# RG-LRU gates of a hybrid decoder block: one matmul per 64-channel block, two blocks in two row groups of the array

## The chip, the cores and the metric

The kernel runs on one core of a Trainium2 chip. The metric is the device time of one launch in microseconds (us). Times of single instructions come from one profiled execution of the kernel; the time that is forecast is the median of unprofiled runs.

## The reference: what is computed

One decoder layer for 1024 tokens of width 1024, all in float32. One input projection feeds three mixers (RWKV-7, RG-LRU, GLA), whose outputs are concatenated into one output projection, followed by a SwiGLU feed-forward part and a final norm. The change touches the gates of the RG-LRU mixer alone:

```python
def rglru_mixer(p, conv_w, conv_b, wa, ba, wx, bx, lam, norm_g):
    xb, gate = _split(p, LRU_SIZES)
    xc = causal_depthwise_conv(xb, conv_w, conv_b)
    xblk = xc.reshape(bsz, t, LRU_BLOCKS, HEAD)
    gate_r = jax.nn.sigmoid(jnp.einsum('btnc,ncd->btnd', xblk, wa).reshape(bsz, t, LRU_WIDTH) + ba)
    gate_i = jax.nn.sigmoid(jnp.einsum('btnc,ncd->btnd', xblk, wx).reshape(bsz, t, LRU_WIDTH) + bx)
    ...
    y = h * jax.nn.gelu(gate.astype(f32))
    y = rms_norm(y.reshape(bsz, t, LRU_BLOCKS, HEAD), norm_g.reshape(LRU_BLOCKS, HEAD))
```

There are 8 blocks of 64 channels. `wa` and `wx` are 64x64 per block, so both gate projections are block-diagonal.

## The kernel before, in words

Channels lie on the 128 partitions, tokens on the free axis, in two halves of 512 tokens. The program has two large stages. In the first (to about 530 us) each half goes through the input projection, the three mixers and the output projection; in the second (to the end) the feed-forward part runs as many 128x512 matmuls (L861, L1124). Weights of the projections come from HBM as float32, are split on ACT and DVE into two parts (`wh`, `wl`, L104 and L105), and each product takes three matmuls (L133, helper `mm3`).

The source gives steps an order (the list `ORDER`, with lead times in `AHEAD`), but what order each engine's instructions stand in is decided by a list scheduler with costs of its own, when the program is built. A change of a few instructions can therefore move many others. All engines then run their queues in that order. SP issues nearly all DMAs.

The RG-LRU mixer is `lru_mix` (L613 and on), called four times: `L00` and `L01` for the first half, `L10` and `L11` for the second, each for two groups of 128 channels (`j` = 0, 1), so for eight groups in all. Each group holds two blocks of 64 channels. For a group the convolution gives `c` (L628 to L630). The gate weights come as a tile `lw` of 128 x 2 x 128 (L625), block-diagonal with zeros outside the two blocks. Two full-array matmuls (L634) give the two gates into two PSUM banks from the pool `px` (two buffers), and one tanh each (L635) takes them out, the first into `y`, the second into the tile `g`. From there ACT and DVE go on: L641, L644, L646, L647, a square root (L649), L650, the scan over tokens (L651), L653, a square (L655), a sum per block on PE (L174), L657; then `lru_fin` (L661, L663, L666), the split of `y` (L104, L105) and the output projection, which reads the RG-LRU channels first (list `KO`).

Float32 matmuls run as two passes on PE; the products of L133 with their split operands run as one. Matmuls that use part of the array are marked in the profile by active rows and columns: `64*128` is half of the rows (one of two row groups) and all columns. `hs(r)` and `ops(r)` are the lower and upper 64 partitions and the reverse.

Of the kernel before, what the change touches and what calls it, by code (L numbers as in the profile page):

```python
# [11 lines left out]
F32 = mybir.dt.float32  # L12
F32R = mybir.dt.float32r
AF = mybir.ActivationFunctionType
# [4 lines left out]
P = 128  # L19
# [49 lines left out]
def hybrid_block(tc, xT, vec, cst, w_in, w_gk, w_ups, lru_w, gk_up, w_out, w_gu, w_dn, outT):  # L69
    nc = tc.nc  # L70
    V, G, S, PE = nc.vector, nc.gpsimd, nc.scalar, nc.tensor

    with ExitStack() as ctx:
# [16 lines left out]
        bah = cp.tile([P, 8], F32, name="bah")  # L90
# [56 lines left out]
        gl = rp.enter_context(tc.tile_pool(name="gl", bufs=1, side="right"))  # L147
# [12 lines left out]
        def mix_ps():  # L160
            return ps_.tile([P, HT], F32, name="px", bufs=2)
# [122 lines left out]
        hs = lambda hh: slice(64 * hh, 64 * hh + 64)  # L284
        ops = lambda hh: slice(64 * (1 - hh), 64 * (1 - hh) + 64)
# [327 lines left out]
        def lru_mix(p, pp, y):  # L613
            it = [(j, 2 * p + j, xb, gate) for j, (xb, gate) in enumerate(pp)]
            out = lambda i: y[:, 2 + i, 3:]
            xc, ig, tt = [], [], []
            for j, i, xb, gate in it:
                ge = unit(2 + j)
                S.activation(out=ge, in_=gate, func=AF.Square, scale=math.sqrt(0.044715))
                plus1(ge, ge, gate)  # L620
                S.activation(out=ge, in_=ge, func=AF.Tanh, scale=math.sqrt(2.0 / math.pi))
                plus1(gate, ge, gate)
            for j, i, xb, gate in it:
                lw = gl.tile([P, 2, P], F32, name="lw", bufs=2)
                nc.sync.dma_start(out=lw, in_=lru_w[:, i])  # L625
                c = unit(j)
                cw = lambda n: vc("cw", 4 * n + i)
                S.activation(out=c, in_=xb[:, 0:HT], func=AF.Identity, bias=vc("cb", i), scale=cw(0))  # L628
                for n in range(1, 4):
                    V.scalar_tensor_tensor(out=c, in0=xb[:, n : n + HT], scalar=cw(n), in1=c, op0=ALU.mult, op1=ALU.add)  # L630
                g = unit(2 + j)
                for w, t, b in ((0, out(i), 0), (1, g, 4)):
                    ps = mix_ps()
                    PE.matmul(out=ps, lhsT=lw[:, w], rhs=c, start=True, stop=True)  # L634
                    S.activation(out=t, in_=ps, func=AF.Tanh, bias=bah[:, b + i : b + i + 1], scale=0.5)  # L635
                plus1(g, g, c)
                xc.append(c)
                ig.append(g)
            for j, i, xb, gate in it:
                t = unit(4 * (1 - j))  # L640
                S.activation(out=t, in_=out(i), func=AF.Tanh, scale=cdec[:, i : i + 1], bias=cdec[:, i : i + 1])  # L641
                tt.append(t)
            for j, i, xb, gate in it:
                S.activation(out=out(i), in_=out(i), func=AF.Exp, scale=ncdec[:, i : i + 1], bias=ncdec[:, i : i + 1])  # L644
                sq = unit(1)
                S.activation(out=sq, in_=out(i), func=AF.Square)  # L646
                V.scalar_tensor_tensor(out=tt[j], in0=sq, scalar=1.0, in1=tt[j], op0=ALU.add, op1=ALU.mult)  # L647
            for j, i, xb, gate in it:
                S.activation(out=tt[j], in_=tt[j], func=AF.Sqrt, scale=0.25)  # L649
                V.tensor_tensor(out=ig[j], in0=ig[j], in1=tt[j], op=ALU.mult)  # L650
                V.tensor_tensor_scan(out=tt[j], data0=out(i), data1=ig[j], initial=lstate[:, i : i + 1], op0=ALU.mult, op1=ALU.add)  # L651
                S.copy(out=lstate[:, i : i + 1], in_=tt[j][:, HT - 1 : HT])
                V.tensor_tensor(out=out(i), in0=tt[j], in1=gate, op=ALU.mult)  # L653
                sq = unit(2 + j)
                S.activation(out=sq, in_=out(i), func=AF.Square)  # L655
                ps = head_sum(sq, blk, mix_ps)
                V.tensor_scalar(out=gate, in0=ps, scalar1=1.0 / 256, scalar2=1e-6, op0=ALU.mult, op1=ALU.add)  # L657
# [421 lines left out]
        for f in range(PRE, NF):  # L1079
            if f >= KF:  # L1080
                r = hidden_room(f - KF)
# [86 lines left out]
        a, b = A.__getitem__, B.__getitem__  # L1168
# [20 lines left out]
        b = B.__getitem__  # L1189
# [53 lines left out]
        r = spread(rstd(Q2, acc1[:, Q2]))  # L1243
# [34 lines left out]
def _lay(i):  # L1278
    f = lambda n: np.asarray(i[n])[0]
    v = np.zeros((P, NV), np.float32)  # L1280

    def put(n, a):
        a = np.asarray(a)
        w = a.size // P
        v[:, VEC[n] : VEC[n] + w] = a.reshape(w, P).T

    put("g1", f("norm1_g"))
    put("g2", f("norm2_g"))
    put("gf", i["final_norm_g"])
    put("mu", f("rw_mu"))  # L1290
    for n, k in (("w0", "rw_w0"), ("a0", "rw_a0"), ("kk", "rw_k_k"), ("ka", "rw_k_a"), ("rk", "rw_r_k"), ("lng", "rw_ln_g"), ("lnb", "rw_ln_b"),
                 ("cw", "lru_conv_w"), ("cb", "lru_conv_b"), ("ba", "lru_ba"), ("bx", "lru_bx"), ("lam", "lru_lam"), ("lg", "lru_norm_g"), ("gkb", "gla_gk_b")):
        put(n, f(k))
    put("gg", np.tile(f("gla_norm_g"), 2))
    v[:, VEC["eps6"]] = 1e-6
    v[:, VEC["epsln"]] = 64e-5
    bp, b4 = np.arange(P) // 32 % 2, np.arange(P) // 8 % 4
    v[:, VEC["hm"] : VEC["hm"] + 2] = np.arange(P)[:, None] // 32 % 2 == np.arange(2)[None]
    v[:, VEC["b0"]] = b4 == 2 * bp
    v[:, VEC["b1"]] = b4 == 2 * bp + 1  # L1300

    w_in = f("w_in")
    swap = lambda w, ax: np.take(w, np.r_[0:64, 128:192, 64:128, 192:256], axis=ax)
    cols = np.concatenate([w_in[:, : 2048 + 512], swap(w_in[:, 2048 + 528 :], 1)], 1)
    tiled = lambda w: np.ascontiguousarray(w.reshape(w.shape[0] // P, P, w.shape[1] // P, P).transpose(2, 1, 0, 3))
    lw = np.zeros((P, 4, 2, P), np.float32)
    for b in range(8):
        s = slice(64 * (b % 2), 64 * (b % 2) + 64)
        lw[s, b // 2, 0, s] = f("lru_wa")[b]
        lw[s, b // 2, 1, s] = f("lru_wx")[b]  # L1310
    return (
        np.ascontiguousarray(np.asarray(i["x"])[0].T).reshape(NK, P, T),
        v,
        _constants(),
        tiled(cols),
        np.ascontiguousarray(w_in[:, 2560:2576].reshape(8, P, 16).transpose(1, 0, 2)),
        np.concatenate([np.concatenate([f("rw_w_up"), f("rw_a_up")], 0), f("rw_g_up")], 1),
        lw,
        np.concatenate([f("gla_gk_up")] * 2, 0),
        tiled(np.concatenate([f("w_out")[:768], swap(f("w_out")[768:], 0)], 0))[:, :, KO],  # L1320
        np.stack([tiled(f("ffn_w_gate")), tiled(f("ffn_w_up"))]),
        np.ascontiguousarray(f("ffn_w_down").reshape(NF, P, NK, P)),
    )
# [15 lines left out]
```

## Time and profile before

| what | before |
|---|---|
| median of 3 runs | 1205.6 us (1205.58 to 1206.74) |
| profiled execution, its own time | 1207.51 us |
| span of that execution | 1205.7 us |
| PE busy | 1159.4 us, 96% of the span |
| DVE, ACT, POOL busy | 820.5, 557.5 and 182.6 us |
| DMA moved | 225.52 MB, 187 GB/s on average |
| mean granted clock of PE | 0.992 |

The span runs from the first to the last instruction; the execution's own time has what lies around it as well, 1.8 us here. Busy shares are averages over stages: what bounds a stage is read from the waits and the order of that stage. A busy PE is the union of its matmul records, whose ends are modelled, so the distance from one start to the next is used below for what a matmul costs.

### The profile page before, as it was taken

Reading aid. Unit: us, or ns where it says so; the run is one execution under the profiler, and the core shown is the slowest. Engines: PE = TensorE matmul, PEld = TensorE weight load, DVE = VectorE, ACT = ScalarE, POOL = GpSimd, SP = SyncE. Lnnn points to the kernel's source line nnn. Section 1 sums busy time; section 2 is a strip of 40 time slices with the busy share of each in tenths; the row PEclk is TensorE's granted clock in tenths of the full one; section 3 lists DMA queues with packets and bytes.
Section 4 is the critical chain, followed back from the end, with each engine's and each line's share of the span. In section 5 each row is a group of like instructions: output and inputs, shape, how many; then the busy total and the mean of one; then the engine's idle time right before and its main releaser. Section 6 shows DMA issues by size and latency. Waiting matters only on the chain.

```text
span 1205.7 us, 18433 instructions
## 1 busy us (share of the span) xinstructions
PE 1159.4 (96%) x6550; PEld 906.5 (75%) x6550; DVE 820.5 (68%) x1513; ACT 557.5 (46%) x972; POOL 182.6 (15%) x141
## 2 busy tenths in 40 slices
PE   8899999999999999988899899999999999999996
PEld 4676667677776677766788778888888878888886
DVE  6878797887759676378978664356655475555775
ACT  7445734864541457365433234333333344444542
POOL 0000000000000000000036455454555400000000
PEclk9999999999999999999999999999999999999998
DMA  9865444343333268873699853245454798665422
GB/s 312 291 231 194 141 147 133 90 157 108 130 123 96 87 219 290 273 258 114 190 324 341 283 194 99 96 131 186 146 176 152 268 357 296 196 194 171 128 88 70
DMA packets 125213, 225.52 MB, mean 187 GB/s; under 512 B 13985, under 2 KB 17345, under 8 KB 125121
## 3 DMA queue, kind: packets, MB, share of 16 engines
q1 hardware_dynamic: 124432, 223.78, 55.1%
q8 instruction: 51, 0.84, 0.3%
q10 hardware_dynamic: 688, 0.57, 0.1%
q14 instruction: 42, 0.34, 0.1%
HBM read 149.84 MB, written 74.45 MB: 186 GB/s over the span
## 4 chain that ended last, share of the span: by engine, by line
PE 62%; DVE 15%; ACT 10%; DMA 9%; issue 3%; SPq 1%; POOL 0%; DVEq 0%; ACTq 0%; POOLq 0%
PE mm L861 24%; PE mm L1124 17%; PE mm L133 12%; DVE x L854 2%; DMA x<-w_dn_dram 2%; DMA wd<-x 1%; PE pi L368 1%; DMA wr<-w_in_dram 1%; DMA wr<-w_gu_dram 1%; ACT L663 1%; DVE wl L105 1%; PE pi L408 1%; DVE x L822 1%; DMA parts<-wl 1%; DVE u L651 1%
## 5 line engine op out<-in xcount | busy, mean ns | idle before, releaser
L133 PE MATMUL mm<-xl,wh 128*128 128x512 f32 x420 | 169.6, 404 | 0.0
L133 PE MATMUL mm<-xh,wh 128*128 128x512 f32 x400 | 162.8, 407 | 3.8 <-ACT wh L104 2.9
L133 PE MATMUL mm<-xh,wl 128*128 128x512 f32 x400 | 163.0, 408 | 0.3 <-DVE wl L105 0.3
L104 ACT CAST wh<-wr 128x512 fp32r<-128x512 f32 x133 | 82.0, 619 | 126.5 <-PE mm L861 37.7
L104 ACT CAST vh<-wr 128x512 fp32r<-128x512 f32 x81 | 50.2, 622 | 103.7 <-PE mm L1124 39.1
L133 PEld LDWEIGHTS mm<-xh,wh 128*128 128x128 f32 x400 | 75.4, 188 | 27.1 <-issue 6.1
L133 PEld LDWEIGHTS mm<-xl,wh 128*128 128x128 f32 x420 | 79.0, 188 | 21.9 <-issue 6.4
L105 POOL TENSOR_TENSOR wl<-wr,wh 128x512 fp32r<-128x512 f32 x36 | 53.0, 1472 | 279.9 <-ACT wh L104 265.2
L133 PEld LDWEIGHTS mm<-xh,wl 128*128 128x128 f32 x400 | 75.3, 188 | 22.6 <-issue 5.8
L1124 PE MATMUL mm<-ft,wh 128*128 128x512 f32 x264 | 81.5, 389 | 0.0
L1124 PE MATMUL mm<-ft,vh 128*128 128x512 f32 x264 | 81.3, 389 | 0.0
L854 DVE TENSOR_TENSOR x<-x 128x512 f32<-128x512 f32 x71 | 57.8, 824 | 29.2 <-DMA x<-hd 15.8
L105 DVE TENSOR_TENSOR wl<-wr,wh 128x512 fp32r<-128x512 f32 x97 | 66.3, 685 | 14.2 <-ACT wh L104 13.7
L417 POOL MEMSET ri<- 128x256 f32 x8 | 2.5, 312 | 391.3 <-DVE ri L402 389.3
L1124 PEld LDWEIGHTS mm<-ft,wh 128*128 128x128 f32 x264 | 49.6, 188 | 10.3
L1124 PEld LDWEIGHTS mm<-ft,vh 128*128 128x128 f32 x264 | 49.5, 188 | 10.2
L105 POOL TENSOR_TENSOR vl<-wr,vh 128x512 fp32r<-128x512 f32 x36 | 50.6, 1406 | 37.6 <-ACT vh L104 36.1
L1124 PE MATMUL mm<-ft,wl 128*128 128x512 f32 x132 | 51.3, 389 | 0.0
L1124 PE MATMUL mm<-ft,vl 128*128 128x512 f32 x132 | 51.3, 389 | 0.0
L104 ACT CAST wh<-ws 128x512 fp32r<-128x512 f32 x33 | 20.4, 622 | 50.9 <-PE mm L861 41.0
L105 POOL TENSOR_TENSOR wl<-ws,wh 128x512 fp32r<-128x512 f32 x27 | 38.4, 1424 | 34.6 <-ACT wh L104 26.9
L105 POOL TENSOR_TENSOR vl<-ws,vh 128x512 fp32r<-128x512 f32 x27 | 37.2, 1376 | 35.7 <-ACT vh L104 35.7
(498 smaller groups left out, 2901.0 us busy)
## 6 DMA issues: line engine op xcount, KB each, us to landing
wr<-w_gu_dram SPq DMA_DIRECT2D x108, 256.0 KB, 3.1
parts<-wh SPq DMA_DIRECT2D x60, 256.0 KB, 3.1
parts<-wl SPq DMA_DIRECT2D x60, 256.0 KB, 3.1
wh<-parts SPq DMA_DIRECT2D x57, 256.0 KB, 2.7
wl<-parts SPq DMA_DIRECT2D x57, 256.0 KB, 2.9
wr<-w_in_dram SPq DMA_DIRECT2D x44, 256.0 KB, 3.9
x<-w_dn_dram SPq DMA_DIRECT2D x44, 256.0 KB, 4.5
wd<-x SPq DMA_DIRECT2D x44, 256.0 KB, 3.9
```

The costliest lines, as they stand in the source:

```text
L104: S.copy(out=hi, in_=src)
L105: lo_eng.tensor_tensor(out=lo, in0=src, in1=hi.bitcast(F32), op=ALU.subtract)
L133: PE.matmul(out=ps, lhsT=ww[:, kk], rhs=xx(k), start=first, stop=last)
L368: PE.matmul(out=pgs[hh][:, n * P : n * P + P], lhsT=BKn[hs(hh), nn, 64 * hh : 64 * hh + 128], rhs=ARn[hs(hh), nn], start=True, stop=True)
L408: PE.matmul(out=ps[hs(hh), n * w : n * w + w], lhsT=lhs(hh, n), rhs=rhs(hh, n), start=True, stop=True)
L417: G.memset(hi(Zt), 0.0)
L651: V.tensor_tensor_scan(out=tt[j], data0=out(i), data1=ig[j], initial=lstate[:, i : i + 1], op0=ALU.mult, op1=ALU.add)
L663: S.activation(out=gate, in_=gate, func=AF.Exp, scale=-0.5)
L822: V.scalar_tensor_tensor(out=xk, in0=xk, scalar=vc("g2", k), in1=rs, op0=ALU.mult, op1=ALU.mult)
L854: eng.tensor_tensor(out=out, in0=a, in1=b, op=op)
L861: PE.matmul(out=ps, lhsT=ww[:, kk], rhs=xx, start=first and kk + i == 0, stop=kk == len(xc) - 1 and i == 2, skip_group_check=True)
L1124: PE.matmul(out=out(m), lhsT=ww[:, m], rhs=xx, start=first and open_(m) and k + i == 0, stop=k == KF - 1 and i == 2, skip_group_check=True)
```

## The change

The weight tile holds 128 x 2 x 64 numbers: the 64 partitions of a block have both of the block's gate matrices side by side in 128 columns (in the upper block in reverse order). Each group of 128 channels now has one matmul per block with 64 rows and 128 columns: block 0 in the lower row group into one bank, block 1 in the upper row group into the other. A bank so holds both gates of one block, each on 64 partitions, and four tanh of 64 partitions take them out in place of two of 128. The tanh of the second gate read the partitions opposite to those they write, since block 0's second gate lies on the upper partitions.

```diff
-                lw = gl.tile([P, 2, P], F32, name="lw", bufs=2)
+                lw = gl.tile([P, 2, 64], F32, name="lw", bufs=2)
                 nc.sync.dma_start(out=lw, in_=lru_w[:, i])
...
                 g = unit(2 + j)
-                for w, t, b in ((0, out(i), 0), (1, g, 4)):
-                    ps = mix_ps()
-                    PE.matmul(out=ps, lhsT=lw[:, w], rhs=c, start=True, stop=True)
-                    S.activation(out=t, in_=ps, func=AF.Tanh, bias=bah[:, b + i : b + i + 1], scale=0.5)
+
+                pg = [mix_ps(), mix_ps()]
+                for r in range(2):
+                    PE.matmul(out=pg[r], lhsT=lw[hs(r)].rearrange("p a b -> p (a b)"), rhs=c[hs(r)], start=True, stop=True)
+                for r in range(2):
+                    S.activation(out=out(i)[hs(r)], in_=pg[r][hs(r)], func=AF.Tanh, bias=bah[hs(r), i : i + 1], scale=0.5)
+                for r in range(2):
+                    S.activation(out=g[hs(r)], in_=pg[r][ops(r)], func=AF.Tanh, bias=bah[hs(r), 4 + i : 5 + i], scale=0.5)
                 plus1(g, g, c)
...
-    lw = np.zeros((P, 4, 2, P), np.float32)
+    lw = np.zeros((P, 4, 2, 64), np.float32)
     for b in range(8):
-        s = slice(64 * (b % 2), 64 * (b % 2) + 64)
-        lw[s, b // 2, 0, s] = f("lru_wa")[b]
-        lw[s, b // 2, 1, s] = f("lru_wx")[b]
+        s, r = slice(64 * (b % 2), 64 * (b % 2) + 64), b % 2
+        lw[s, b // 2, r] = f("lru_wa")[b]
+        lw[s, b // 2, 1 - r] = f("lru_wx")[b]
```

In the changed kernel the matmuls are on L635 and the tanh on L637 and L639; lines behind them are four higher. The order of the instructions moves on PE, DVE, ACT and SP from early in the input projection to some way into the feed-forward part; behind that it is the same.

**Order 1.** PE, the first group of `L00`, in the midst of the input projection (L133; L378 transposes one row group for RWKV). Before, and then of the change:

```order
L133 MATMUL mm<-xh_155,wh 128x512
L133 MATMUL mm<-xl_156,wh 128x512
L634 MATMUL px<-u_1163,lw 128x512 x2
L378 MATMUL pi<-ct,BK 128x64 x8
L133 MATMUL mm<-xh_155,wl 128x512
```

```order
L133 MATMUL mm<-xl_152,wh 128x512
L133 MATMUL mm<-xh_151,wl 128x512
L635 MATMUL px<-u_1163,lw 128x512 x2
L133 MATMUL mm<-xh_155,wh 128x512
L133 MATMUL mm<-xl_156,wh 128x512
```

The two gate matmuls follow each other in both; they now stand alone between full-array matmuls.

**Order 2.** PE, the last group of `L11`, shortly before the output projection of the second half. Before, and then of the change:

```order
L634 MATMUL px<-u_4897,lw 128x512
L133 MATMUL mm<-xh_4258,wh 128x512
L133 MATMUL mm<-xl_4259,wh 128x512
L133 MATMUL mm<-xh_4258,wl 128x512
L133 MATMUL mm<-xh_4262,wh 128x512
L634 MATMUL px<-u_4897,lw 128x512
```

```order
L635 MATMUL px<-u_4911,lw 128x512
L133 MATMUL mm<-xl_4271,wh 128x512
L133 MATMUL mm<-xh_4270,wl 128x512
L133 MATMUL mm<-xh_4274,wh 128x512
L133 MATMUL mm<-xl_4275,wh 128x512
L635 MATMUL px<-u_4911,lw 128x512
```

Four full-array matmuls stand between the two gate matmuls in both.

**Order 3.** ACT, the two groups of `L11`. Before, and then of the change:

```order
L635 ACTIVATE y_101<-px,bah 128x512
L641 ACTIVATE u_4910<-y_101,cdec 128x512
L635 ACTIVATE u_4887<-px,bah 128x512
L644 ACTIVATE y_101<-y_101,ncdec 128x512
L104 CAST wh<-wr 128x512
L635 ACTIVATE y_101<-px,bah 128x512
L641 ACTIVATE u_4912<-y_101,cdec 128x512
L644 ACTIVATE y_101<-y_101,ncdec 128x512
L635 ACTIVATE u_4902<-px,bah 128x512
```

```order
L637 ACTIVATE y_101<-px,bah 64x512
L639 ACTIVATE u_4899<-px,bah 64x512
L637 ACTIVATE y_101<-px,bah 64x512
L639 ACTIVATE u_4899<-px,bah 64x512
L645 ACTIVATE u_4926<-y_101,cdec 128x512
L104 CAST wh<-wr 128x512
L648 ACTIVATE y_101<-y_101,ncdec 128x512
L637 ACTIVATE y_101<-px,bah 64x512
L639 ACTIVATE u_4916<-px,bah 64x512
L637 ACTIVATE y_101<-px,bah 64x512
L639 ACTIVATE u_4916<-px,bah 64x512
```

Four tanh of 64 partitions now stand where two of 128 stood, and the next step of the group (L641, now L645) comes behind all four, where it came behind the first.

## Rows read from the trace of the kernel before

**Rows 1.** Busy us by stretch: PE, PEld, DVE, ACT, POOL; clock, DMA share, GB/s.
```profile
60.00:460.00 400.00, 394.06 (x3083) 285.72 (x3082) 309.97 (x721) 208.77 (x353) 2.50 (x8) 1.00 0.44 146
460.00:500.00 40.00, 39.06 (x215) 29.98 (x214) 24.78 (x44) 22.86 (x32) 0.00 (x0) 1.00 0.76 257
...
530.00:600.00 70.00, 57.99 (x236) 45.55 (x235) 63.67 (x105) 38.70 (x66) 0.00 (x0) 0.95 0.46 149
...
700.00:1205.00 505.00, 492.01 (x2293) 411.40 (x2291) 289.48 (x430) 203.66 (x367) 132.25 (x99) 0.99 0.52 172
```
**Rows 2.** PE's waits from 60 to 460: us in total, times, longest.
```profile
PE pi L301 <- DVE Tt L426: 1.6, 2, 1.1
...
PE px L174 <- ACT u L655: 0.3, 1, 0.3
```
**Rows 3.** Timeline of PE around the first gate matmuls: start us, us, instruction, count.
```profile
84.67 1.88 PE L634 MATMUL px<-u,lw 128*128 128x512 f32 x4
86.49 0.71 PE L378 MATMUL pi<-ct,BK 64*128 64x64 f32 x8
```
**Rows 4.** Timeline of PE where two matmuls of each row group meet, RWKV's L301 and L309.
```profile
26.43 0.48 PE L301 MATMUL pi<-pw,ups 64*128 64x256 f32 x1 [0.77 <-ACT pw L279]
26.44 0.48 PE L309 MATMUL pi<-pw,ups 64*128 64x256 f32 x1
26.75 0.38 PE L301 MATMUL pi<-pw,ups 64*128 64x256 f32 x1
...
26.96 0.37 PE L301 MATMUL pi<-pw,ups 64*128 64x256 f32 x1
...
27.18 0.38 PE L301 MATMUL pi<-pw,ups 64*128 64x256 f32 x1
...
27.50 0.50 PE L133 MATMUL mm<-xh,wl 128*128 128x512 f32 x1
27.83 0.39 PE L133 MATMUL mm<-xh,wh 128*128 128x512 f32 x1
28.06 0.40 PE L133 MATMUL mm<-xl,wh 128*128 128x512 f32 x1
```
**Rows 5.** Timeline of PE where a row group begins behind the input projection.
```profile
337.94 0.39 PE L133 MATMUL mm<-xh,wl 128*128 128x512 f32 x1
338.26 1.13 PE L309 MATMUL pi<-pw,ups 64*128 64x256 f32 x4
```
**Rows 6.** Tanh of 128 and of 64 partitions by line: ns min/median/max, first and last start.
```profile
L635 ACT ACTIVATE y<-px,bah x8: 668/678/711, 86.1 to 455.3; 128x512 f32<-128x512 f32 x8
L279 ACT ACTIVATE pw<-pw x2: 612/622/632, 25.7 to 230.6; 64x512 f32<-64x512 f32 x2
```
**Rows 7.** A group of table loads on ACT: busy us, mean ns, idle before.
```profile
L649 ACT ACT_TABLE_LOAD x4 | 5.1, 1283 | 0.1
```
**Rows 8.** Timeline of ACT, last group of `L11` to its split `y`.
```profile
455.28 0.68 ACT L635 ACTIVATE y<-px,bah 128x512 f32<-128x512 f32 x1
...
470.71 0.63 ACT L655 ACTIVATE u<-y 128x512 f32<-128x512 f32 x1 [1.19 <-DVE y L653]
...
481.95 0.62 ACT L104 CAST y<-y 128x512 fp32r<-128x512 f32 x1 [0.82 <-DVE y L666]
```
**Rows 9.** Timeline of PE: that group's sum, and the first matmul reading its `y`.
```profile
473.74 1.02 PE L174 MATMUL px<-u,ct 128*128 128x512 f32 x2
...
484.69 0.39 PE L133 MATMUL mm<-y,wh 128*128 128x512 f32 x1
```
**Rows 10.** The start by stretch, columns as in rows 1.
```profile
20.00:30.00 10.00, 9.19 (x42) 6.49 (x40) 6.61 (x14) 6.63 (x14) 0.00 (x0) 1.00 1.03 356
30.00:40.00 10.00, 7.26 (x24) 4.97 (x24) 5.09 (x12) 7.03 (x14) 0.00 (x0) 0.83 0.86 313
```
**Rows 11.** DMA issues: queue, count, KB each, us to landing.
```profile
lw<-lru_w_dram SPq DMA_DIRECT2D x8, 128.0 KB, 2.3
```
**Rows 12.** PE's waits from 530 to 600, columns as in rows 2.
```profile
PE mm L861 <- ACT ft L803: 4.2, 1, 4.2
PE mm L861 <- DVE q_t2l L105: 3.3, 2, 1.8
```

## The prediction, made before the changed kernel ran

> **What bounds the kernel now.** I read the table of busy time by stretch first, since the change lies between 60 and 460 us. PE is busy in 394.06 of those 400 us, in 39.06 of the next 40, and in 492.01 of the last 505 [rows 1]. PE is the bound nearly everywhere. The exception is 530 to 600 us, the opening of the feed-forward part, where PE has 57.99 of 70 us and DVE 63.67, and the mean granted clock is 0.95 [rows 1]: two waits of 4.2 and 3.3 us stand there [rows 12]. Then I read PE's waits in the stretch of the change: the largest is 1.6 us, for RWKV, and its wait for an RG-LRU result is 0.3 us in all [rows 2]. ACT is busy in 208.77 of those 400 us [rows 1]. So a pass taken from PE is worth its own time, and work added to ACT is hidden as long as PE still has other matmuls queued ahead of what waits for it. Last I read the timelines for prices.
>
> **PE: the passes.** The two gate matmuls of a group are four passes of 512 columns; from the first to the next work is 86.49 - 84.67 = 1.82 us [rows 3], of which about 0.09 is the change of tiling priced below, so 0.43 us a pass and 1.73 us a group. The trace has a pair in two row groups, at 256 columns: L301 and L309 start 0.01 us apart, and each stream goes on every 0.22 us as if alone [rows 4]. At 512 columns I take 0.43 us a pass, two passes side by side, 0.87 us a group, if the two matmuls stand next to each other. They do in six of the eight groups, as in order 1; each saves 0.86 us, 5.2 us in all. In the last group they are four matmuls apart, as in order 2, and nothing overlaps. In one group of `L01` a matmul of another tiling (L450) stands between them; the second then runs beside L301, which before ran beside L309, so nothing is gained there either. Passes: -5.2 us.
>
> **PE: the changes of tiling.** Going into a row group and coming back is not free. From the last L133 to the first tiled pass it is 338.26 - 337.94 = 0.32 us [rows 5], where two L133 lie 0.23 apart [rows 4]; from the first to the second tiled pass it is 0.32 where the next are 0.22 apart; from the last tiled pass to L133 it is 0.32 in place of 0.22; from that L133 to the next 0.33 in place of 0.23 [rows 4]. That is four times 0.10, so 0.2 us for each change of tiling. I counted, over the whole PE order, the places where one matmul's tile size differs from the one before: 252 before, 275 now. Of the 23 more, 14 come from the gates (order 1 shows a pair that now has one on either side), and 9 from other tiled matmuls that the scheduler put in other places. 23 x 0.2 = +4.6 us. Passes and tiling together: -0.6 us. Most of what the row groups give is taken back.
>
> **ACT.** A tanh of 64 partitions takes 0.62 us, one of 128 takes 0.68 [rows 6]; half the partitions save next to nothing. So 32 for 16 adds 16 x 0.65 = 10.4 us, and ACT's order has three more table loads (58, was 55) of 1.28 us each [rows 7], 3.9 us. These 14.3 us have PE's work as cover: ACT has nearly half of the stage free. Where the cover is thin, the next step of the group waits for two more tanh, 1.3 us (order 3), the casts of weights (L104) that PE needs are queued behind them, and both `px` banks are held until the third and fourth tanh, so the next group's gate matmuls wait longer. The thinnest place I found is behind `L11`. Before, the square of the last group was done at 470.71 + 0.63 = 471.34 and PE took it up at 473.74, 2.4 us later; its `y` was split at 482.57 and read at 484.69, 2.1 us later [rows 8, 9]. With the same prices PE's order now holds 1.2 us less work between the last gate matmul and the first one that reads that `y` (27.1 us, was 28.3). So 2.1 us of slack meet 1.2 + 1.3 us: a wait of 0.4 us. The other three calls lie amid the input projection. I take +1.5 us for all four. Bounds: 0, if all is covered, and 4 x 1.3 = 5.2, if each call shows one group's delay.
>
> **DMA.** Each of the eight loads of `lw` is 64 KB in place of 128 [rows 11]. Two are issued at the start, where the DMA engines are full (1.03 and 0.86 of their time, at 356 and 313 GB/s) and PE is not (9.19 and 7.26 of 10) [rows 10]: 131 KB at 356 GB/s is -0.4 us. The other six are hidden. SP issues as many DMAs as before. DVE and POOL have the same instructions.
>
> **The moved order.** Almost every engine's order moves, the opening of the feed-forward part too. I take 0 for it. The two waits there [rows 12] may each go or grow, and the clock's 0.95 over 70 us is some 7 us at 1.2 GHz, 3.5 us lost [rows 1]; I bound the term by 4 us either way.
>
> **Sum**: -0.6 + 1.5 - 0.4 + 0 = +0.5 us. The profiled execution took 1207.5 us, which would become 1208.0; the median of the runs shown is 1205.6, 1.9 lower, so I forecast 1206.1. A measurement of this kernel tells about 0.2% from no change, 2.4 us: no change is 1203.2 to 1208.0.
>
> **Rivals.**
> - *Faster, because changing the tiling costs nothing.* All eight groups save 0.86 us, 6.9 in all, with the DMA's 0.4: 1198.3. For it: the two streams really run side by side [rows 4]. Against it: the four 0.10 us around them [rows 4, 5], and order 2. The Trainium skill, page "TensorE: Matmul & The Clock Gate", section "Measured speedup vs the span model", prices a pack at one matmul and about 4 ns for each further tile; by it this rival would hold. The trace agrees on the start (0.01 us) and not on what stands before and behind.
> - *Faster by the moved order.* Waits at the opening of the feed-forward part shrink, or the slow-clock stretch goes: 4 us less, 1202. Nothing in the profile speaks for one sign.
> - *Slower, because the row groups don't overlap: the change doesn't do what it says.* If matmuls start strictly in order, the second block's first pass waits for the first block's second, and a pair takes three passes in place of two: 6 x 0.43 = 2.6 us given back, 1208.7. It decides if the second block starts a whole pass behind. Against it: both L301 matmuls stand ahead of both L309 in PE's order, and L309 still started 0.01 us behind the first pass of L301 [rows 4]. The Trainium skill, same page, section "The mechanism", states that matmuls start and end in strict order, with no reordering; by it this rival would hold, and the row disagrees.
> - *Slower, because the gate chain becomes the bound.* The place is behind the gates of each call, above all `L11`; the price is 5.2 us in place of 1.5, so 1209.8. It decides where the added tanh and the shorter cover pass the slack of 2.1 to 2.4 us [rows 8, 9]. For it: the slack is small, and the scheduler laid it out by its own costs. Against it: PE's 0.3 us of waiting for this chain [rows 2].
> - *Slower by the moved order*, at the same place as its faster twin: 4 us more, 1210.
>
> **How the numbers follow.** Forecast (within 0.2%): 0.40. Free tiling 0.10 and a luckier order 0.15 make faster 0.25. No overlap 0.05, gate chain 0.20 and a worse order 0.10 make slower 0.35. The range takes the sum with the order's 4 us either way and a part of the gate chain's bound above: 1201.0 to 1211.0; free tiling, and both upper bounds at once, lie outside.
>
> **What would show it.** Right: gate passes (64*128) that start in pairs 0.01 us apart in six groups, 0.43 us from pass to pass; 0.3 us steps into and out of them; 32 tanh near 0.65 us; ACT busier by 14 us; PE's waits for RG-LRU results between 60 and 500 us up by 1 to 2 us. Wrong: pairs 0.43 us apart (no overlap), steps of 0.23 us (free tiling), or a wait above 2 us at L174 or at the first output matmuls of the second half (gate chain). If the time moves by more than 2.4 us and the stretch before 500 us doesn't account for it, the moved order was mis-sized.

## The result: 1218.1 us, 1% slower

| | before | changed |
|---|---|---|
| median (range) | 1205.6 us (1205.37 to 1214.22, 7 runs) | 1218.14 us (1214.55 to 1225.71, 7 runs) |
| ratio, 95% interval | | 1.0094 [1.0064, 1.0123] |
| profiled execution, its span | 1207.51, 1205.7 us | 1214.97, 1213.2 us |
| PE, ACT busy | 1159.4, 557.5 us | 1163.9, 574.0 us |
| mean granted clock | 0.992 | 0.984 |

The forecast was 1206.1 (1201 to 1211); the measured time lies 7 us above the range. In the table of stretches of the changed kernel (columns of rows 1) the loss stands in the stretch of the change:

```profile
60.00:460.00 400.00, 386.83 (x3035) 279.39 (x3035) 302.92 (x714) 212.01 (x352) 2.49 (x8) 0.97 0.42 137
460.00:500.00 40.00, 39.70 (x214) 27.68 (x212) 27.93 (x50) 31.06 (x48) 0.00 (x0) 1.00 0.70 241
...
530.00:600.00 70.00, 61.06 (x249) 47.05 (x247) 63.73 (x104) 40.93 (x69) 0.00 (x0) 0.95 0.47 147
700.00:1205.00 505.00, 496.89 (x2316) 415.56 (x2314) 289.80 (x430) 204.93 (x369) 132.64 (x98) 1.00 0.53 175
```

From 60 to 460 us PE is now busy in 386.83 us, 7.2 less than before, and the clock's mean fell from 1.00 to 0.97 [rows 1]. The opening of the feed-forward part, where the prediction looked for a moved order, has the same 0.95. PE's waits from 60 to 460 us, the longest five (columns of rows 2):

```profile
PE mm L133 <- DVE pw L252: 4.2, 1, 4.2
PE pc L445 <- DVE rwS L458: 2.5, 1, 2.5
PE mm L133 <- ACT u L659: 2.2, 1, 2.2
PE px L174 <- ACT u L659: 2.0, 1, 2.0
PE pp L465 <- DVE UV L451: 1.3, 1, 1.3
```

Before, the longest there was 1.1 us [rows 2]. Two of the five name the RG-LRU's last square (L659, L655 before): PE's wait for RG-LRU results is 4.2 us in all, where it was 0.3 [rows 2] and 1 to 2 more were forecast. The other three, 8.0 us, belong to RWKV's chain and to the norm of the second half, where the diff changes nothing; they stand together between 222 and 232 us. PE's timeline there (columns of rows 3; in brackets the idle time ahead and what ended it):

```profile
221.59 0.45 PE L450 MATMUL pc<-R,Tt 64*64 64x64 f32 x8 [0.18 <-DVE R L447]
223.39 0.33 PE L465 MATMUL pp<-XR,UV 128*64 128x64 f32 x2 [1.35 <-DVE UV L451]
...
226.85 0.69 PE L445 MATMUL pc<-rwS,AR 64*64 64x64 f32 x8 [2.45 <-DVE rwS L458]
231.74 0.79 PE L133 MATMUL mm<-xh,wh 128*128 128x512 f32 x1 [4.20 <-DVE pw L252]
232.33 0.63 PE L133 MATMUL mm<-xl,wh 128*128 128x512 f32 x1
232.76 0.63 PE L133 MATMUL mm<-xh,wl 128*128 128x512 f32 x1
```

The second and the third L133 behind the hole lie 0.43 us apart, where two of them lay 0.23 apart before [rows 4]: the granted clock was at its lower level, 1.2 GHz. Busy time and clock of this stretch, before and then changed (columns of rows 1):

```profile
220.00:235.00 15.00, 14.18 (x76) 9.39 (x75) 13.26 (x25) 14.59 (x23) 0.00 (x0) 1.00 0.37 114
```
```profile
220.00:235.00 15.00, 6.82 (x44) 4.54 (x43) 11.63 (x24) 11.08 (x15) 0.00 (x0) 0.66 0.00 0
```

ACT's timeline tells what came late, first before, then changed:

```profile
222.19 0.67 ACT L136 ACTIVATE rstd<-pi,vt 128x512 f32<-128x512 f32 x1
222.88 1.28 ACT L137 ACT_TABLE_LOAD   x1
224.18 0.63 ACT L137 ACTIVATE rstd<-rstd 128x512 f32<-128x512 f32 x1
```
```profile
226.70 0.69 ACT L136 ACTIVATE rstd<-pi,vt 128x512 f32<-128x512 f32 x1
227.41 1.28 ACT L597 ACT_TABLE_LOAD   x1
228.70 1.06 ACT L597 ACTIVATE u_qk<-u_qk 128x1024 f32<-128x1024 f32 x1
229.66 0.61 ACT L137 ACTIVATE rstd<-rstd 128x512 f32<-128x512 f32 x1
```

`rstd`, which every projection of the second half is multiplied by, was ready at 224.81 us and is now ready at 230.27, and none of the split tanh stands in this stretch: the scheduler put other work ahead. Before, PE had nineteen products of the input projection between 217 and 225 us to cover the norm; now the last of them is issued at 216.4, and the next L133 is the one at 231.74. So two suspects were left, the **order** and the **parts** (32 tanh for 16, the changes of tiling).

### The profile page after: what moved, and what is told of

The parts are those of the page before. It is cut to its first block, busy times and chain, and to the rows that moved or that the text cites. A ratio compares the mean times of both kernels' runs of the same rounds, so it can differ in the third digit from the quotient of the medians.

```text
span 1213.2 us, 18465 instructions
## 1 busy us (share of the span) xinstructions
PE 1163.9 (96%) x6550; PEld 907.2 (75%) x6550; DVE 819.5 (68%) x1513; ACT 574.0 (47%) x991; POOL 179.3 (15%) x141
## 4 chain that ended last, share of the span: by engine, by line
PE 71%; DVE 10%; DMA 8%; ACT 7%; issue 3%; SPq 1%; DVEq 0%; ACTq 0%
PE mm L865 23%; PE mm L133 19%; PE mm L1128 17%; DMA wr<-w_gu_dram 3%; DMA x<-w_dn_dram 2%; DVE x L858 2%; PE pi L408 2%; PE pi L368 1%; DMA wd<-x 1%; DVE ws L858 1%; DVE x L826 1%; PE px L570 1%; DMA y<-xT_dram 1%; DVE wl L105 1%; PE px L174 1%
## 5 line engine op out<-in xcount | busy, mean ns | idle before, releaser
L133 PE MATMUL mm<-xh,wh 128*128 128x512 f32 x400 | 164.7, 412 | 7.8 <-DVE pw L252 4.2
L133 PE MATMUL mm<-xl,wh 128*128 128x512 f32 x420 | 170.7, 406 | 0.0
L133 PE MATMUL mm<-xh,wl 128*128 128x512 f32 x400 | 161.2, 403 | 1.6 <-DVE wl L105 1.6
L133 PEld LDWEIGHTS mm<-xh,wh 128*128 128x128 f32 x400 | 76.5, 191 | 30.9 <-issue 6.4
L133 PEld LDWEIGHTS mm<-xl,wh 128*128 128x128 f32 x420 | 80.4, 191 | 24.5 <-issue 8.3
L133 PEld LDWEIGHTS mm<-xh,wl 128*128 128x128 f32 x400 | 76.5, 191 | 22.3 <-issue 4.1
```

The lines of the kernel that those rows point to most:

```text
L133: PE.matmul(out=ps, lhsT=ww[:, kk], rhs=xx(k), start=first, stop=last)
```

## The experiments

Two tools serve most of them. **A held order**: for each engine the order of another kernel's program is read out and laid on this kernel's instructions by edges that fix the order of issue and add no wait. (Before's order laid on the change lets each gate tanh of before stand for two.)

```diff
+ISSUE = {"PE": "...", "DVE": "...", "Activation": "...", "Pool": "...", "SP": "..."}
...
+        order = [v[k] for k in struct.unpack("<%dH" % len(v), raw)]
+        for a, b in zip(order[:-1], order[1:]):
+            tc.add_manual_dep(b, a.name, mybir.DependencyInfo(mybir.DependencyClass.NoSync, mybir.DependencyReason.DATA), reason="issue order")
```

**Span times clock.** Every run lists its span and the mean granted clock. Their product is the span less half of the time at half clock; I call the rest *lost*. It is an upper bound of the clock's price, since a wait is no shorter at full clock. The clock is listed to a thousandth, which is 1.2 us of lost time, and single runs of one kernel scatter (span times clock from 1198.1 to 1205.5 in e3's six), so a difference of about 2 us between two rows is weak. Medians, in us:

| kernel | median | ratio [95%] | span x clock | lost |
|---|---|---|---|---|
| before (94 runs in all) | 1206 to 1207 | 1 | 1193.9 | 10.8 |
| changed | 1218.1 | 1.0094 [1.0064, 1.0123] | 1197.0 | 18.2 |
| e1 change, old order | 1220.6 | 1.0102 [1.0076, 1.0129] | 1202.2 | 15.8 |
| e2 before, new order | 1217.7 | 1.0086 [1.0057, 1.0115] | 1196.1 | 20.0 |
| e3 tanh split alone, old order | 1218.8 | 1.0089 [1.0063, 1.0115] | 1202.7 | 13.4 |
| e4 row groups alone, old order | 1209.8 | 1.0017 [0.9996, 1.0038] | 1191.7 | 16.9 |
| e7 tanh split in L01 alone | 1211.0 | 1.0033 [1.0010, 1.0056] | 1196.9 | 12.1 |
| e10 tanh split in the other calls | 1216.9 | 1.0081 [1.0051, 1.0110] | 1197.7 | 17.6 |
| e9 small lw alone, free order | 1219.9 | 1.0132 [1.0093, 1.0171] | 1201.2 | 18.3 |
| e13 before, old order to 240 us | 1209.7 | 1.0006 [0.9986, 1.0027] | 1194.6 | 14.5 |
| e14 change, old order to 240 us | 1216.5 | 1.0081 [1.0053, 1.0109] | 1197.7 | 18.2 |
| e15 before, new order to 200 us | 1208.6 | 0.9991 [0.9968, 1.0014] | 1188.0 | 18.1 |
| e17 e15 kept busy | 1201.4 | 0.9951 [0.9933, 0.9970] | 1191.6 | 8.4 |

### e1 to e4: order and parts, each alone

**e1**, the change in the old order:

> The changed kernel's instructions (two row-group matmuls, four 64-partition tanh, small lw), with every engine held by issue-order edges to the order of the kernel before (each gate tanh of before stands for two). Table loads are 55 as before, tile-size changes on PE 266 (252 before, 275 in the changed kernel). Order theory (the 9 to 12 us come from the order into which the scheduler moved the work, through holes on PE and the half clock after them): 1203 to 1208 us, within 0.3% of before. Parts theory (the new instructions themselves cost it: longer gate chain on ACT, tile-size changes on PE): 1214 to 1220 us, about 1% slower than before.

**e2**, before in the new order:

> The instructions of the kernel before (full-array gate matmuls, one tanh per gate, 128 KB lw), with every engine held to the issue order of the changed kernel. Order theory: 1213 to 1219 us, about 0.8 to 1.1% slower than before, with PE holes near 109, 225 to 232 and 265 us and the clock falling behind them. Parts theory: 1204 to 1208 us, the time of before.

Measured: 1220.6 and 1217.7. Each theory was right in the half that it claimed and wrong in the other. The new order alone costs before 0.86%, and the parts alone cost 1.02% in the old order. e1 lies 0.6 us above the range of the parts theory. The two costs don't add up: together they are 0.94%, so in the new order the parts add nothing that these intervals can tell. Of what they cost in the old order, the largest piece (`L01`, below) seems covered in the new one: ACT sits idle ahead of that call's first tanh, waiting for PE, which comes out of its hole at 231.74.

```profile
239.28 0.68 ACT L637 ACTIVATE y<-px,bah 64x512 f32<-64x512 f32 x1 [3.21 <-PE px L635]
```

The tanh still show in PE's two waits for the RG-LRU's square, 1.2 and 1.0 us in e2 and 2.2 and 2.0 in the changed kernel. That these 2 us are paid for by the row groups (2.2 us by e4) fits the numbers, but no run separates it.

**e3**, the tanh alone:

```diff
-                    S.activation(out=t, in_=ps, func=AF.Tanh, bias=bah[:, b + i : b + i + 1], scale=0.5)
+                    for r in range(2):
+                        S.activation(out=t[hs(r)], in_=ps[hs(r)], func=AF.Tanh, bias=bah[hs(r), b + i : b + i + 1], scale=0.5)
```

> Before, in its own order, with only the two gate tanh of a block split into four of 64 partitions (the matmuls full-array). The prediction's term for the 16 more tanh: +1.5 us (0 to 5.2). Order theory: 1205.5 to 1208. Parts theory with the gate chain as cause: 1213 to 1218. Parts theory with the PE side as cause: 1205 to 1207.

**e4**, the row groups alone (the edit is shown against the changed kernel):

```diff
-                for r in range(2):
-                    S.activation(out=out(i)[hs(r)], in_=pg[r][hs(r)], func=AF.Tanh, bias=bah[hs(r), i : i + 1], scale=0.5)
-                for r in range(2):
-                    S.activation(out=g[hs(r)], in_=pg[r][ops(r)], func=AF.Tanh, bias=bah[hs(r), 4 + i : 5 + i], scale=0.5)
+                for r, t, b in ((0, out(i), 0), (1, g, 4)):
+                    S.activation(out=t, in_=pg[r], func=AF.Tanh, bias=bah[:, b + i : b + i + 1], scale=0.5)
```

> Before, in its own order, with only the gate matmuls made into two row-group matmuls with the small lw; the two tanh read 128 partitions of each product, so the gates of every second block are exchanged and the output is another (same amount of work). Tile-size changes on PE 266 against 252: 14 x 0.2 = +2.8 us; the pairs save at most 8 x 0.86 = 6.9, of it 5.2 if only the adjacent six do; DMA 0.4 less. Prediction's terms: 1202 to 1205. Parts theory with the PE side as cause: 1212 to 1218. Parts theory with the gate chain as cause, and order theory: 1202 to 1206.

e3: 1218.8, as slow as the whole change and 0.8 us above the range for the gate chain. e4: 1209.8, above 1202 to 1206 and below 1212 to 1218, so outside what every theory had said; its ratio is no measurable difference from before. By span times clock it is 2.2 us shorter, but it lost 6.1 more to the clock. So of the parts the tanh cost, not PE. Why they cost shows on ACT in `L01`, before and then e3 (its L636 is L635 of before; the count is of the tanh in a row):

```profile
231.69 0.67 ACT L635 ACTIVATE y<-px,bah 128x512 f32<-128x512 f32 x1
...
233.95 0.67 ACT L635 ACTIVATE u<-px,bah 128x512 f32<-128x512 f32 x1
...
235.95 0.71 ACT L635 ACTIVATE y<-px,bah 128x512 f32<-128x512 f32 x1
...
240.56 0.66 ACT L635 ACTIVATE u<-px,bah 128x512 f32<-128x512 f32 x1
...
241.98 0.63 ACT L646 ACTIVATE u<-y 128x512 f32<-128x512 f32 x1 [0.36 <-DVE u L611]
```
```profile
233.57 1.36 ACT L636 ACTIVATE y<-px,bah 64x512 f32<-64x512 f32 x2
...
236.64 1.38 ACT L636 ACTIVATE u<-px,bah 64x512 f32<-64x512 f32 x2
...
239.48 1.38 ACT L636 ACTIVATE y<-px,bah 64x512 f32<-64x512 f32 x2
...
244.59 1.38 ACT L636 ACTIVATE u<-px,bah 64x512 f32<-64x512 f32 x2
...
246.72 0.63 ACT L647 ACTIVATE u<-y 128x512 f32<-128x512 f32 x1 [0.23 <-DVE u L611]
```

e3 comes into this stretch 1.88 us late (233.57 against 231.69) and leaves it 4.74 late (246.72 against 241.98). The difference, 2.86 us, is four times 0.7, the four added tanh: ACT has hardly a gap here, in before as in e3, because RWKV's preparation of the next chunk stands between the gates. Over 400 us ACT was busy in half of the time [rows 1]; over these 10 it was full.

### e7, e10: which call's tanh

> Before, in its own order, with the gate tanh split into two of 64 partitions in the call L01 alone (4 more tanh of 16). In e3 ACT worked without a gap from 229 to 242 us and everything behind came 2.9 us later, 4 x 0.70. If the split tanh lengthens a chain that nothing covers there: 2.0 to 2.9 us by itself, up to 5 with a further fall of the clock: 1208.5 to 1212 us. If the tanh are covered as the prediction had it (1.5 us for all 16, so 0.4 for 4): 1206 to 1207.5.

> Before, in its own order, with the gate tanh split in the calls L00, L10 and L11 (12 more tanh), the complement of e7. By span times granted clock, e3 was 8.8 us over before and e7 3.0. If the direct cost adds up by calls: 5.8 (4 to 7) by span times clock here, and 1211 to 1217 us. If it is the sum of ACT's work that counts and not the place: 6.6 (three quarters of 8.8). If L01 alone matters: 0 to 1, and 1206 to 1208 us.

The edit is that of e3 under a condition on the call (`y is y0 and p == 1`, or its opposite). By span times clock e7 is +3.0 us for its four tanh, the 4 x 0.7 of the timeline, and e10 +3.8 for its twelve, a little under the low end of what was expected. Per tanh `L01` costs 0.75 us and the others 0.3, so the place counts and not the number alone. Their sum, 6.8, is less than e3's 8.8; the last 2.0 I can't assign, and they are within the scatter. Where the twelve cost shows in PE's waits from 60 to 500 us, first before (beside the 0.3 us for L655 [rows 2]), then e10 (its L656 and L693 are L655 and L692 of before):

```profile
PE mm L133 <- DVE rt L692: 0.9, 1, 0.9
```
```profile
PE px L174 <- ACT u L656: 2.9, 2, 2.4
PE mm L133 <- DVE rt L693: 2.4, 1, 2.4
```

The wait of 0.3 us is the one at the sum of `L10` (ended at 322.76 us); it is 2.4 in e10 and in e3. The one for L692 stands at the first output matmuls of the second half (486.49 us), where DVE comes to the addition that empties a bank only behind the RG-LRU results of `L11` (L666). Together these two grew by 3.6 us, near the 3.8.

### e9, e11: a moved order by itself

**e9** halves the load of `lw` and leaves everything else, and the scheduler is free:

```diff
-                lw = gl.tile([P, 2, P], F32, name="lw", bufs=2)
+                lw = gl.tile([P, 2, 64], F32, name="lw", bufs=2)
...
-                    PE.matmul(out=ps, lhsT=lw[:, w], rhs=c, start=True, stop=True)
+                    PE.matmul(out=ps, lhsT=lw.rearrange("p a b -> p (a b)"), rhs=c, start=True, stop=True)
```

> Before with only the load of the gate weights halved (64 KB; both gate products of a block then use the same 128 columns, so the gates are others), and nothing held: the scheduler moves 1547 of 5507 matmuls for it, nearly as many as for the whole change. No tanh, no tile size and no matmul is different. If the cost of the change lies in having lost the order of before, whatever moved it: 1211 to 1219 us. If a moved order costs nothing by itself and the split tanh are what costs: 1204 to 1208.

1219.9 us, 0.9 above the first range: 64 KB less to load, eight times, and the kernel is 1.3% slower. The load itself isn't to blame, since e4 has the same one in the old order. PE's longest wait between 200 and 240 us, and the stretch (before: 39.18 of 40 us busy, clock 1.00):

```profile
PE px L634 <- DVE u L630: 5.0, 1, 5.0
```
```profile
200.00:240.00 40.00, 32.37 (x332) 20.46 (x332) 26.34 (x53) 24.75 (x38) 0.62 (x2) 0.83 0.13 43
```

The hole lies at the same place (it ends at 229.98 us), with another wait on top. **e11**, the changed kernel with `"L10": 1500` in the table of priorities:

> The changed kernel with one number of the table of priorities moved (L10 from 1000 to 1500), nothing held: another order of the same instructions (742 of 5507 matmuls stand elsewhere). Order theory (a moved order is worth several us either way): outside 1216 to 1220, by 3 us or more, up or down. Parts theory: 1216 to 1220 us, the changed kernel's time.

1219.3, ratio 1.0121 [1.0086, 1.0157]: another order, not another time, so the parts theory's number held. But the same waits of 4.2 and 2.5 us are in it: this order kept the place that costs. How an order without it would do, e11 can't tell.

### e13 to e15: the place of the moved order

Set the start of each matmul against the summed prices of those ahead of it (an estimate; the price is the median step from start to start in before). All four kernels with a moved order (the change, e2 with its order, e9, e11) are 3 to 4 us ahead of before at 200 us and 6 to 9 behind at 240: they lose 10 to 12 us there, more than anywhere else. These three join the two orders, engine by engine: what one order issues up to a moment, then the rest in the other's order.

> The instructions of before, held to the order of before for what it issues in its first 240 us, and to the order of the changed kernel behind that. If the moved order costs at one place, between 205 and 235 us: 1203 to 1207.5 us, the time of before. If it costs all along: 1210 to 1218.

> The instructions of the change, held in the same way: old order to 240 us, new order behind it. The eight split tanh of L00 and L01 cost about 3 (e7), the row groups give 1 to 2 back, and the second half is in the order that the scheduler made for the split tanh. If the place between 205 and 235 us is what the new order costs: 1206 to 1213 us. If the split tanh cost as much in the new order's second half as in the old one (e10): 1214 to 1219.

> The instructions of before, held to the order of the changed kernel for what that issues in its first 200 us, and to the order of before behind that. If the hole of 222 to 232 us comes of what was done earlier (PE some 3 us ahead, the products that cover the norm of the second half used up): 1211 to 1218 us with that hole. If it comes of the order between 200 and 240 us itself (the two instructions of rstd, the products placed behind them): 1203 to 1208.

e13: ratio 1.0006, so nothing behind 240 us costs that shows (its median of 1209.7 is over the expected range; the runs of before beside it had 1207.0). e15: 0.9991 (1208.6, 0.6 over the range), and of the hole nothing is left: the longest wait from 200 to 240 us is one of 1.7. So of the three pieces of the new order only the one from 200 to 240 us is left to cost, and what was issued earlier doesn't make the hole. That piece alone in the old order wasn't run. e15 is 5.8 us better than before by span times clock and lost 7.3 more to the clock, in the profiled run most of it behind that wait of 1.7 us, just behind the joint. e2's 2.2 us by span times clock then looks like a balance: about 8.0 of waits between 222 and 232 us against 5.8 won earlier.

e14: 1216.5, the second range. But the calls `L00` and `L01` lie in its part with the old order, where `L01` alone costs 3.0 (e7), and by span times clock it is 3.1 over e13. How much the split tanh cost in the new order's second half is not separated.

### e8: one cause too few

The lines of ACT's instructions there, in the changed kernel and then in e8:

```order
L595 L628 L595 L619 L621 L136 L597 L137 L621
L595 L628 L136 L137 L595 L619 L621 L597 L621
```

> The changed kernel in its own order on every engine, but for two instructions of ACT: the two of the norm of the second half (logarithm and exponential of rstd, lines 136 and 137) stand next to each other, behind the first logarithm of G0, as in before, not third and fifth behind it. Order theory (the moved order made the hole of 4.2 us at 231.7 and the half clock of 224.5 to 234.7 behind it): 1211 to 1215 us, 3 to 6 less than the changed kernel. If what is won there is lost at the next hole: 1216 to 1219.

1222.9, ratio 1.0130 [1.0094, 1.0167], above both ranges; by span times clock it is 1196.4, as the change (1197.0), and it lost 24.5 to the clock. `rstd` was ready at 226.81 in place of 230.27, but PE's wait for `rwS` grew from 2.5 to 6.2 us. DVE's timeline tells why:

```profile
229.35 0.69 DVE L611 SCALAR_TENSOR_TENSOR u<-u,ga 128x512 f32<-128x512 f32 x1 [2.97 <-ACT u L619]
...
232.00 0.48 DVE L458 SCALAR_TENSOR_TENSOR rwS<-pc,PC,SP 128x64 f32<-128x64 f32 x2
...
233.59 0.69 DVE L252 TENSOR_TENSOR pw<-mm,rstd 128x512 f32<-128x512 f32 x1
```

In DVE's list the RG-LRU's L611 stands ahead of RWKV's `rwS` and of `pw`, and L611 waits for the L619 that I had pushed back; DVE stood idle for 2.97 us and took nothing from behind it. Three engines wait for each other here, and mending the order of one of them moved the wait to another.

### e5, e6, e12, e16, e17: the clock

These add matmuls of no use ahead of a waiting one, into a bank that the next real matmul overwrites or nobody reads:

```diff
+        def warm(ps, n):
+            w = min(384, ps.shape[1])
+            for _ in range(n):
+                WARM.add(PE.matmul(out=ps[:, :w], lhsT=ones, rhs=ct[:, CST["ones"][0] : CST["ones"][0] + w], start=True, stop=True).ins.name)
```

> Before, in its own order, with 5 matmuls of no use (f32, 128x384, into the bank that the next real matmul overwrites) in the 4.2 us hole of PE ahead of the first FFN product, and 2 in the 1.5 us hole ahead of the norm behind it. If the clock falls because PE stands still there, most of the 6.9 us at half clock behind the hole of 538 us (worth 3.4) goes: 1201.5 to 1204.5 us. If the hole has nothing to do with the clock, or the useless matmuls only stand in the way: 1206 to 1209.

> The kernel of e1 with the same useless matmuls as e5, and also 4 (128x256) in its hole at 114 us (ahead of the first level's second product of b0) and 3 (128x384) in its hole at 333 us (ahead of the first head sum of L10). Clock theory (of e1's 13.9 us over before about 10 are the half clock behind holes, by the trace 3.2 at 114, 1.5 at 333, 3.4 at 554 and 565): 1209 to 1215 us. Theory that the longer gate chain costs it by waits alone: 1218 to 1224.

> The changed kernel held to its own order, with useless matmuls in four of its holes: 8 and 16 (128x128, into a part of the chain's bank that nobody uses) in the holes of 2.45 us at 226.9 and 4.2 us at 231.7, 2 (128x384) in that of 2.0 us at 264.7, 5 in that of 4.4 us at 557.6. The waits themselves stay. Clock theory (the half clock behind a hole comes from PE standing still): the falls at 224.5, 265.5 and 555.6 shrink or go, worth 1.8 + 1.7 + 3.4 at most: 1211 to 1215 us, span times clock as before within 1.5 us. If the clock falls for another reason: 1217 to 1221.

e5: 1208.2, 1.0017 [0.9999, 1.0036]. The useless matmuls waited 4.1 us for the same bank as the real one and filled nothing; the hole that ends at 538 us was a wait for DVE to empty that bank. e12: 1219.6, 1.0117 [1.0085, 1.0149]. Its first eight waited 2.5 us, as the real ones had, then stood in their way. The other places did fill, and the clock rose there (220 to 240 us: 0.74 to 0.91; 262 to 275: 0.87 to 1.00; 553 to 565: 0.72 to 1.00). It lost 15.8 where the change lost 18.2, but span times clock is 1201.1, 4.1 more, so nothing was won. e6 worked at its two first places. e1, then e6, at 110 and at 328 us:

```profile
110.00:122.00 12.00, 9.24 (x100) 6.46 (x98) 7.82 (x12) 5.46 (x10) 0.00 (x0) 0.72 0.33 108
328.00:340.00 12.00, 9.26 (x113) 5.90 (x113) 8.20 (x13) 8.16 (x12) 0.00 (x0) 0.86 0.19 66
```
```profile
110.00:122.00 12.00, 10.97 (x124) 7.08 (x123) 8.76 (x14) 7.54 (x12) 0.00 (x0) 1.00 0.35 119
328.00:340.00 12.00, 11.37 (x125) 6.57 (x125) 7.49 (x12) 8.87 (x12) 0.00 (x0) 1.00 0.15 45
```

With PE kept at work the clock stayed at full in both. Yet e6 took 1223.1, 1.0134 [1.0105, 1.0163]: it lost 16.5 to the clock, as e1 did (15.8), now at later holes, among them that of e5, and by span times clock it is 3.1 over e1.

> Before in its own order with 6 useless matmuls (f32, 128x384, some 0.65 us each) ahead of the first FFN product, into a bank that nothing waits for, so that PE works through 3.9 of the 4.2 us of that hole. Clock theory: no half clock behind 538 us, 2 to 3.4 us less: 1202 to 1204 us. If the clock falls there all the same: 1205 to 1208.

In e16 the bank was free, and the fill was real. Before, then e16:

```profile
530.00:545.00 15.00, 10.82 (x37) 8.40 (x35) 13.58 (x23) 7.95 (x15) 0.00 (x0) 0.77 0.49 166
```
```profile
530.00:545.00 15.00, 12.98 (x50) 8.80 (x48) 13.98 (x24) 7.20 (x12) 0.00 (x0) 1.00 0.54 178
```

The clock didn't fall there, and the profiled run has a span of 1202.4. Over twelve runs the ratio is 0.9994 [0.9972, 1.0015], the second range: the next wait, 1.5 us at 548.7 before, is 3.3 us in e16, and the clock fell there in its place.

> The kernel of e15 (instructions of before, new order to 200 us, old order behind it) with 3 useless matmuls (f32, 128x256) in its hole of 1.7 us at 205 us and the 6 of e16 ahead of the first FFN product. If the falls behind these two holes are what eats the 5.8 us: span times clock 1187 to 1190, lost to the clock 11 to 13 instead of 18, and 1200 to 1203.5 us, better than both kernels. If the clock falls at other holes instead, as in e16: 1204 to 1208, no better than before.

e17: 1201.4 us (1200.45 to 1203.19), faster than both kernels, with the narrowest range of all that ran six times or more. Against before it has 2.3 us less by span times clock and 2.4 less lost. From 200 to 230 us, e15 and then e17:

```profile
200.00:230.00 30.00, 28.27 (x293) 20.73 (x291) 18.99 (x40) 16.11 (x26) 0.00 (x0) 0.72 0.10 34
```
```profile
200.00:230.00 30.00, 28.75 (x338) 20.38 (x334) 23.27 (x48) 21.04 (x34) 0.00 (x0) 1.00 0.19 66
```

In e15 a hole of 1.7 us was followed by half clock from 205 to 222 us. Filled, it is not, and the lost time goes from 18.1 to 8.4. The time came as expected, but by other sizes: span times clock 1191.6 where 1187 to 1190 was expected, lost 8.4 where it was 11 to 13. At the second place e17 does what e16 did: the next wait is 3.2 us (at 543.6) and the clock falls there. So it is probably the first fill that makes the difference; e15 with that fill alone wasn't run. The Trainium skill, page "TensorE: Matmul & The Clock Gate", section "Why this matters for your kernels", advises against long idle gaps of PE between bursts of matmuls. e15 and e17 go further, with 0.72 and 1.00 in these rows: here a hole of 1.7 us was enough.

## Why the prediction was wrong, point by point

- **What bounds the kernel.** "Work added to ACT is hidden as long as PE still has other matmuls queued ahead of what waits for it": right as a sentence, but judged by busy time over 400 us. In the 10 us round the gates of `L01` ACT was full (e3, e7). The 3.3 us that it calls one wait at the opening of the feed-forward part are two, the longest 1.8 [rows 12].
- **PE's passes and tiling, -0.6.** Right in its prices; no run measures the term in the new order. In six groups the pairs are adjacent. One group of the changed kernel:

```profile
78.26 0.39 PE L133 MATMUL mm<-xh,wl 128*128 128x512 f32 x1
78.58 1.13 PE L635 MATMUL px<-u,lw 64*128 64x512 f32 x4
79.64 0.50 PE L133 MATMUL mm<-xh,wh 128*128 128x512 f32 x1
79.97 0.39 PE L133 MATMUL mm<-xl,wh 128*128 128x512 f32 x1
```

  The step in is 0.32 us and the one behind it 0.33, as priced; the group takes 1.06 us, where the step into the next work was 1.82 [rows 3]. e4 gives the sum in the old order: 266 changes of tiling against 252, and in its trace five pairs, not six, start together (both groups of `L01` stand apart). By the prediction's prices that is -5 x 0.86 + 14 x 0.2 = -1.5, with the DMA's 0.4 it is -1.9, and -2.2 by span times clock. Free tiling asks for steps of 0.23 us where 0.32 and 0.33 stand, so that rival falls; four passes of 0.43 us in 1.06 do overlap, so the third rival falls too.
- **ACT, +1.5 (0 to 5.2).** This step failed. The price of one tanh was right:

```profile
L637 ACT ACTIVATE y<-px,bah x16: 668/684/688, 79.7 to 472.1; 64x512 f32<-64x512 f32 x16
L639 ACT ACTIVATE u<-px,bah x16: 670/680/688, 83.0 to 472.8; 64x512 f32<-64x512 f32 x16
```

  0.68 us where 0.65 was taken, and ACT is 16.5 us busier (14.3 forecast). What showed was mis-sized: +8.8 us by span times clock in the old order (e3), past the upper bound of 5.2, which had one group's delay (two tanh) for each call; `L01` alone was delayed by four tanh, 2.86. And it was not one place. "The thinnest place I found is behind `L11`", and that did cost: the wait for L692 grew by 1.5. But `L01` cost 3.0 (e7) and the wait of `L10` grew by 2.1 (e10), where "the other three calls lie amid the input projection". The "0.3 us of waiting for this chain" [rows 2], which the prediction put against the gate-chain rival, was the sign for it: PE already waited for the RG-LRU at `L10`, so no cover was left there. That rival was right in kind for the old order, with too small a price, and its sign (a wait above 2 us at L174 or at the first output matmuls of the second half) is there in e3.
- **DMA, -0.4.** No run measures it as a transfer; as a number in the scheduler's reckoning it moved the order, and that alone costs 1.3% (e9).
- **The moved order, 0 (up to 4 either way).** The step that failed for the kernel as it stands: e2 measures +0.86%, some 10 us, 2.2 by span times clock and up to 9.2 by the clock. The prediction bounded it at the opening of the feed-forward part alone, where the waits were already large, and not where they would arise: at 222 to 232 us, in a stretch where before's longest wait was 0.8 us. The changed order has L136 and L137 apart there (e8); I read the order only round the gates. The range's lower end, 1201.0, lies 1.1 below what the sum and the 4 us give; that changed nothing.
- **The clock.** Taken as a trait of one place. The changed kernel spends 30.7 us at half clock ahead of its last 15 us, where before has 10.3.

The rival "slower by the moved order" (0.10) is what happened in the changed kernel, at another place and with some 10 us (e2) in place of 4.

## What to carry to other kernels

A change that a scheduler sees, even the size of one load, is a change of the whole order; hold the order fixed in one run and move it alone in another before a cost or a gain is put down to the edit. Judge cover in windows as long as the work that is added, and on every queue of the loop of engines that wait for each other, not by a stage's busy share. Where PE is the bound, list the granted clock with the time: a wait of 1.7 us had 17 us at half clock behind it (e15), and an edit that saved 2.2 us of PE's work lost 6.1 to the clock (e4).

## What was not expected of the hardware

- The clock falls behind some short holes and not behind others of about the same size, and not in every run of one kernel. In the changed kernel it fell behind one of 2.2 us at 109 us and not behind one of 1.95 that ends at 536; in e7 it was at half from 371 to 384 us, and PE's busy time from 365 to 390 is 24.15 us, as in before, where it stayed at full. The lost time of before's own 94 runs goes from 7.2 to 20.6 us at the same order. What decides it stays open.
- Keeping PE at work at one hole moved the falls to others (e6, e16). Only e17, which also filled the hole with the longest stretch at half clock behind it, became faster and steadier as a whole.
- A tanh of 64 partitions out of PSUM takes 0.68 us, whether it writes to the partitions that it reads (L637) or to the other half (L639): as long as one of 128 [rows 6], so splitting it by partitions doubles its time on ACT.
